# An added GpSimd drain in the tail of a 2x2 average-pooling kernel

## Chip, cores, metric

One core of a Trainium2 chip. The metric is the device time of one execution in microseconds; lower is better. All runs quoted are with a granted clock of 1.00.

## The reference

Average pooling with a 2x2 window and stride 2 on float32, 32 x 128 planes of 256 x 256, to 128 x 128 each.

```python
def setup_inputs():
    return {'x': np.random.randn(32, 128, 256, 256).astype(np.float32), 'kernel_size': 2, 'stride': 2}

def reference(x, kernel_size, stride):
    ...
            window = x[:, :, h_start:h_start + kernel_size, w_start:w_start + kernel_size].copy()
            output[:, :, i, j] = np.mean(window, axis=(2, 3))
```

1073.7 MB are read and 268.4 MB written.

## The kernel before

Each engine has its own program, tied to the others by semaphores. SyncE and ScalarE load (each the half of a tile), VectorE adds, ScalarE multiplies by 0.25, and GpSimd issues 62 stores of 4 MB each. The last 4 MB pair of tiles is stored by SyncE and the rest behind it in four smaller stores by ScalarE. The parts that matter here, with comments added:

```python
    def store(k, c):
        take(pool, scaled, 2)
        pool.dma_start(out=op[k], in_=both[c].rearrange("p t g f -> p (t g f)")).then_inc(stored[c], 16)

    def emptied_by(c, landed):
        pool.wait_ge(stored[c], landed)      # the store has landed ...
        pool.sem_inc(emptied[c])             # ... and VectorE may fill the buffer again

    with tc.tile_critical():
        # (cut: SyncE's loads, VectorE's and ScalarE's programs, the last five stores)

        store(0, 0)
        with pool.Fori(0, (pairs - 3) // 2) as i:
            for c in (1, 0):
                store(2 * i + (2 - c), c)
                emptied_by(1 - c, 16 * i + 16)
        store(pairs - 2, 1)
        for c in range(2):
            emptied_by(c, 16 * (pairs - 1) // 2)

        take(sp, tail, 16 * (len(parts) + 2))   # SyncE: all five last stores have landed
```

At the end of the critical section (line 135 in the profile) the framework makes SyncE release the other engines; each then executes a drain instruction that reports back to SyncE, and a barrier over all engines ends the program (line 290; 291 where the kernel is a line longer).

## Time and profile before

| | before |
|---|---|
| time, median of 4 runs | 3108.21 us (3107.80 to 3108.42) |
| span of the profile | 3106.8 us |
| mean DMA rate over the span | 432 GB/s |
| last landing, seen by SyncE | 3100.8 us |
| GpSimd's drain of line 135 | 3100.9 to 3106.0 us, 5127 ns |

The kernel is limited by its transfers for all but its last 6 us. In rows of a line's instructions, the columns are the line, the engine (a `q` at the end is its sequencer), the operation and how often, the durations in ns as min/median/max, and the first and last start in us. A row of the waits has the waiting engine and line, for whom, total us, times, longest us.

### The profile page before, as it was taken

To read this page: it belongs to the slowest core of one execution; us is meant where nothing else is said; L and a number is where in the kernel's file an instruction comes from. 1 tells how busy PE (TensorE), PEld (TensorE's weight loads), DVE (VectorE), ACT (ScalarE), POOL (GpSimd) and SP (SyncE) were. 2 spreads that over 40 slices of the span, in tenths; PEclk is the share of its full clock that TensorE was granted. 3 is DMA by queue.
4 is the path that set the end of the run, shared out by engine and by line. 5 is a ranking of instruction groups with operands and counts; after the bars stand their busy time and mean duration, and the time that the engine had idled before them with its cause. 6 is when DMAs were issued, how large, how long until landed. Compare 5 with 4: busy or idle time off the path is not lost. (4 is left out here: it accounts for less than half of the span.)

```text
span 3106.8 us, 2727 instructions
## 1 busy us (share of the span) xinstructions
DVE 1679.3 (54%) x260; ACT 503.1 (16%) x161; POOL 38.0 (1%) x66
## 2 busy tenths in 40 slices
DVE  5555555555555555555555555555555555555555
ACT  1111111111111111111121111211111111211111
POOL 0000000000000000000000000000000000000000
DMA  9999999999999999999999999999999999999998
GB/s 419 432 436 434 432 432 438 426 437 438 434 426 442 429 432 435 435 439 432 435 435 427 435 435 433 432 438 439 432 432 437 428 438 432 439 426 435 440 433 373
DMA packets 30449, 1342.21 MB, mean 432 GB/s; under 512 B 5232, under 2 KB 5232, under 8 KB 5488
## 3 DMA queue, kind: packets, MB, share of 16 engines
q10 hardware_dynamic: 10976, 541.07, 40.3%
q1 hardware_dynamic: 10544, 541.07, 40.2%
q0 software_dynamic: 8928, 260.05, 19.4%
q14 instruction: 1, 0.01, 0.0%
HBM read 1073.74 MB, written 268.44 MB: 432 GB/s over the span
## 5 line engine op out<-in xcount | busy, mean ns | idle before, releaser
L108 DVE TENSOR_TENSOR in_tile<-in_tile 128x8192 f32<-128x8192 f32 (+1 forms) x130 | 1112.9, 8561 | 1390.9 <-DVEq L79 1390.9
L119 ACT ACTIVATE res<-res 128x4096 f32<-128x4096 f32 x127 | 459.3, 3616 | 1975.7 <-ACTq L79 1952.0
L110 DVE TENSOR_TENSOR res<-in_tile 128x4096 f32<-128x4096 f32 x127 | 561.9, 4425 | 18.6
L119 ACT ACT_TABLE_LOAD x31 | 39.8, 1283 | 604.3 <-ACTq L79 604.3
L129 POOL DMA_DIRECT2D out_dram<-res x62 | 37.8, 610 | 2971.1 <-POOLq L79 2971.1
L119 ACT ACTIVATE in_tile<-in_tile 128x1024 f32<-128x1024 f32 (+1 forms) x3 | 4.0, 1341 | 7.3 <-ACTq L79 7.3
L110 DVE TENSOR_TENSOR in_tile<-in_tile 128x1024 f32<-128x1024 f32 (+1 forms) x3 | 4.7, 1581 | 0.4
L276 POOL MEMSET const-float32-0.0<- 128x1 f32 x1 | 0.1, 93 | 0.4 <-issue 0.4
L276 POOL MEMSET const-bfloat16-1.0<- 128x1 bf16 x1 | 0.1, 95 | 0.0
L276 POOL MEMSET const-float32-1.0<- 128x1 f32 x1 | 0.1, 93 | 0.0
L276 POOL MEMSET const-uint8-127<- 128x1 uint8 x1 | 0.1, 93 | 0.0
## 6 DMA issues: line engine op xcount, KB each, us to landing
out_dram<-res POOLq DMA_DIRECT2D x62, 4096.0 KB, 49.9
out_dram<-res SPq DMA_DIRECT2D x1, 4096.0 KB, 33.6
in_tile<-in_x_dram ACTq DMA_DIRECT2D x1, 2048.0 KB, 15.4
in_tile<-in_x_dram SPq DMA_DIRECT2D x1, 2048.0 KB, 18.1
in_tile<-in_x_dram ACTq DMA_DIRECT2D x2, 1024.0 KB, 23.1
in_tile<-in_x_dram SPq DMA_DIRECT2D x2, 1024.0 KB, 23.2
out_dram<-res ACTq DMA_DIRECT2D x1, 2048.0 KB, 16.3
in_tile<-in_x_dram ACTq DMA_DIRECT2D x127, 32.3
```

Of the source, the lines that this page charges most:

```text
L108: dve.tensor_add(out=it[:, :, 0:w], in0=it[:, :, 0:w], in1=it[:, :, w:]).then_inc(halfway)
L110: dve.tensor_add(out=dst, in0=it[:, :, 0:w:2], in1=it[:, :, 1:w:2]).then_inc(summed)
L119: act.mul(out=dst, in_=dst, mul=0.25).then_inc(sem)
L129: pool.dma_start(out=op[k], in_=both[c].rearrange("p t g f -> p (t g f)")).then_inc(stored[c], 16)
L276: nc = _bacc.Bacc("TRN2", target_bir_lowering=False, num_devices=1)
```

## The change

GpSimd knows that its last store has landed some 42 us before the others are done: in the profile before, its last wait for a store (line 133) passes at 3058.6 us, and SyncE sees the last landing at 3100.8.

```profile
L133 POOLq EVENT_SEMAPHORE  x62: 17/17/17, 111.9 to 3058.6; - x62
```

`pool.drain()` is the instruction that the framework gives GpSimd at line 135. The intent is to let GpSimd drain once in those 42 us already, and not only when SyncE releases it at the end.

```diff
         store(pairs - 2, 1)
         for c in range(2):
             emptied_by(c, 16 * (pairs - 1) // 2)
+        pool.drain()
```

## The prediction

> **What bounds the kernel now.** I read the page from its top first: busy times, the DMA row, the queues.
>
> ```profile
> span 3106.8 us, 2727 instructions
> DVE 1679.3 (54%) x260; ACT 503.1 (16%) x161; POOL 38.0 (1%) x66
> ...
> DMA  9999999999999999999999999999999999999998
> GB/s 419 432 436 434 432 432 438 426 437 438 434 426 442 429 432 435 435 439 432 435 435 427 435 435 433 432 438 439 432 432 437 428 438 432 439 426 435 440 433 373
> ...
> HBM read 1073.74 MB, written 268.44 MB: 432 GB/s over the span
> ```
>
> No engine is busy for more than 54%; the 16 DMA engines are busy in every slice and move 432 GB/s. Each byte of x is read once and each byte of the output written once, so 39 of the 40 slices are transfers. Only the last slice (373 GB/s) holds time that is not, and the change sits there. So the second reading is the end, with the chain that ended last, the waits of SyncE, and the DMA view of the last 7 us.
>
> The chain that ended last is of no help: it stops at the last ScalarE operation, 16 us before the span's end, because what follows are waits, stores and drains and not counted work. The waits of SyncE from 3050 us on carry the argument:
>
> ```profile
> SPq L79 <- SPq L79: 69.6, 3, 40.7
> SPq L135 <- POOLq L135: 4.9, 1, 4.9
> SPq L290 <- PEq L290: 0.6, 2, 0.4
> ```
>
> Each row is who waited, for whom, total, times, longest. The 40.7 us is SyncE waiting for the five last stores, up to 3100.8 us, where the output is complete. After that it waits 4.9 us for GpSimd at line 135, the end of the critical section. The instructions of that line, and of line 290, which closes the program, say what GpSimd does then (durations in ns min/median/max, then the first and last start in us):
>
> ```profile
> L135 SPq EVENT_SEMAPHORE  x3: 17/17/28, 3100.8 to 3101.1; - x3
> L135 SPq NOP  x2: 13/13/13, 0.9 to 3106.0; - x2
> L135 ACTq DRAIN  x1: 8/8/8, 3100.9 to 3100.9; - x1
> L135 POOLq DRAIN  x1: 5127/5127/5127, 3100.9 to 3100.9; - x1
> L135 DVEq DRAIN  x1: 10/10/10, 3100.9 to 3100.9; - x1
> L135 SPq DRAIN  x1: 7/7/7, 3100.9 to 3100.9; - x1
> ...
> L290 POOLq EVENT_SEMAPHORE  x4: 17/17/17, 3106.2 to 3106.7; - x4
> L290 POOLq DRAIN  x3: 34/34/77, 3106.1 to 3106.6; - x3
> L290 SPq DRAIN  x3: 7/7/7, 3106.1 to 3106.4; - x3
> ...
> L290 ACTq DRAIN  x2: 8/70/132, 3101.3 to 3106.4; - x2
> ```
>
> Four engines drain at the same moment; three need 7 to 10 ns and GpSimd 5127 ns. SyncE's NOP, which lets the program go on, starts at 3106.0 when that drain ends. So some 5 us at the end of 3108 are one GpSimd instruction in which nothing is moved: the DMA view of 3100 to 3107 us shows three packets, 0.01 MB, none on GpSimd's queue.
>
> **What the Trainium skill says.** "PSUM — Partial Sum Buffer", section "Engine vs sequencer instructions": "drain waits for the engine to go fully idle". The trace agrees in part only. GpSimd's last DMA instruction starts at 3008.9 us and takes 0.6, its last store has landed by 3058.6 us (the last wait of line 133 passes there), so by what is recorded it had been idle for 42 us when the drain began, and still it took 5.1 us. "Perfetto Trace Analysis", section "Sequencer-only Instruction (DRAIN, etc)": the reported time starts once the semaphores are satisfied. The trace agrees: the drain starts within 0.1 us of SyncE's release at 3100.8 us, and the 40 us of waiting before it are not in it; so 5127 ns is execution. "VectorE: DVE Perf Modes", section "The DRAIN you can't avoid", gives some 12 ns for a boilerplate drain on every engine: that fits 7 to 10 ns here, and not GpSimd's 34 to 5127. "DMA: Bandwidth & Descriptors", section "SWDGE vs HWDGE vs iDMA": for GpSimd's transfers software on its cores writes descriptors into rings in SBUF. No page says what a drain does with these rings. My reading, inferred, is that the first drain after transfers does overdue bookkeeping for the 62 stores of queue 0, whether or not they have landed.
>
> **The change part by part.** It removes nothing and moves nothing that exists. The built programs differ in one instruction: GpSimd has one drain more, behind its wait for the last store (line 133, at 3058.6 us) and in front of the branch out of the critical section; the drain at line 135 stays. No semaphore, transfer or tile changes, and the increment that VectorE waits for is given before the new drain.
>
> 1. The added drain. By the one measured duration it takes 5.1 us, from 3058.6 to about 3063.7 us. GpSimd has nothing to do until SyncE releases it at 3100.9 us: 42.3 us of room, 37 us of it left over. Cost on the path: 0. It could be eight times slower and stay hidden.
>
> 2. The drain at line 135. If the new one has done the bookkeeping, it costs what GpSimd's drains right after the long one cost: 34, 34 and 77 ns. It then ends at 3100.9 + 0.08, about 3101.0 us and not 3106.0.
>
> 3. What sets the end then? Not 5127 - 77 = 5050 ns saved in full, as two others come into view. SyncE's own semaphore instructions of line 135 run until 3101.1 us and its NOP follows them, so from this side the NOP moves from 3106.0 to 3101.1: 4.9 us, the wait that the row of SyncE shows. Then line 290's barrier gathers all engines. Before, the last to come was SyncE's drain, at about 3106.17 us, right after the NOP. ScalarE's first drain of line 290 starts at 3101.3 us and takes 132 ns, so it arrives at about 3101.41. It did not wait for GpSimd, so it won't be earlier. The gather is complete at 3101.4 and not at 3106.17: 4.76 us are saved. The rest of the barrier, 3106.2 to 3106.8, moves along unchanged.
>
> Sum: 3108.37 + 0 - 4.76 = 3103.61 us, 0.15% less. The span of the profile should go from 3106.8 to about 3102.0.
>
> **The rivals.** (a) The cost comes back: a drain's 5.1 us belongs to any drain of GpSimd after a long idle time, or to the one at a critical section's end, and not to unfinished bookkeeping. Then the second drain costs 5.1 us again after its 37 us of rest and the time stays 3108.4. For it: the three short drains follow the long one within 0.6 us, so none shows what a rest does. Against it: after 46 to 61 us of rest GpSimd's DMA instruction takes 608 ns, 725 at most, so waking up costs 0.1 us at best; and GpSimd's drain at the program's start, before any store, took 184 ns with four memsets around it. I give it 15%.
>
> (b) The drain waits for something outside GpSimd: for instance for all DMA engines to be quiet, or for the one packet of instruction fetch (8 KB on queue 14) that the DMA view shows between 3100 and 3107 us. If it waited for all DMA traffic, the new drain would last till about 3100.8 us, when the last store lands, and the old one would be short if nothing else remained: still near 3103.6; if 5 us must follow the last landing, nothing is gained. Against it: at 3100.9 us all transfers had landed, and the fetch is one 8 KB packet of 0.4 us that starts a microsecond into the drain. With 5%, half of it no gain.
>
> (c) The early drain disturbs what runs beside it. From 3058.6 to 3063.7 us SyncE issues the last large store and VectorE starts a tile; a drain that touches SBUF or the DMA rings could slow these. The store's issue was 0.6 us and its landing is waited for at the very end with the other stores, behind some 40 us of transfers, so even 1 us lost would be lost in full: 3104.6. I see no such sign in the trace; 10%.
>
> (d) Partly sticky: the second drain costs 1 to 2 us. Then 3104.5 to 3105.5; 5%.
>
> **Range and chances.** The middle is 3103.6. The runs of before lie within 0.37 us, and the new instruction stands behind the steady part, so I allow 1.2 us of noise downwards; upwards the range takes in (c) and (d) but not (a). So 3102.4 to 3105.8, which holds about 8 times in 10, as (a) and half of (b) take some 17%. No reading yields 2% (62 us): the whole stretch behind the last landing is 6 us. Within 2% gets 0.994, and 0.003 each side for surprises.
>
> **What would show it right or wrong.** In the profile after: a GpSimd drain on the new line, starting near 3058.6 us and near 5100 ns long (step 1); the drain of line 135 under 100 ns (step 2); SyncE's wait for GpSimd at line 135 gone or under 0.1 us, ScalarE the last at the barrier of line 290, the span near 3102.0 us (step 3). Right for the wrong reason would be a new drain that lasts until 3100 us, rival (b). Wrong it is if the drain of line 135 is still near 5 us (a), or if the last store lands later than 3100.8 us (c).

## The result, and the profile after

The changed kernel takes 3103.57 us, median of four runs (3103.24 to 3103.69), against 3108.21 us: 4.64 us less, or 0.15%. The ratio is 0.9985, with a 95% interval of 0.9968 to 1.0002. The span of the profile is 3102.0 us.

The new instruction and the lines at the end, in the profile after:

```profile
L197 POOLq DRAIN  x1: 5127/5127/5127, 3058.2 to 3058.2; - x1
```

```profile
L135 SPq NOP  x2: 13/13/13, 0.9 to 3101.1; - x2
L135 ACTq DRAIN  x1: 8/8/8, 3100.8 to 3100.8; - x1
L135 POOLq DRAIN  x1: 34/34/34, 3100.8 to 3100.8; - x1
```

```profile
L291 POOLq EVENT_SEMAPHORE  x4: 17/17/17, 3101.4 to 3101.9; - x4
L291 POOLq DRAIN  x3: 34/34/78, 3100.9 to 3101.8; - x3
L291 SPq DRAIN  x3: 7/7/7, 3101.2 to 3101.6; - x3
...
L291 ACTq DRAIN  x2: 8/70/132, 3101.3 to 3101.6; - x2
```

The reader is to see the same 5127 ns, to the nanosecond, on the new line 197 at 3058.2 us, and 34 ns in its old place. SyncE's NOP starts at 3101.1 and not at 3106.0 us. In the last fence GpSimd's semaphore instruction, which gathers the barrier, passes at 3101.4 us, when ScalarE's 132 ns drain that started at 3101.3 has ended. The waits of SyncE from 3050 us on have lost one row:

```profile
SPq L79 <- SPq L79: 69.6, 3, 40.7
SPq L291 <- PEq L291: 0.7, 2, 0.4
```

The 40.7 us for the last stores is what it was; the 4.9 us of waiting for GpSimd is gone.

### The profile page after: what moved, and what is told of

It is laid out like the page before. It is cut to its first block, busy times and chain, and to the rows that moved or that the text cites. A ratio compares the mean times of both kernels' runs of the same rounds, so it can differ in the third digit from the quotient of the medians.

```text
span 3102.0 us, 2728 instructions
## 1 busy us (share of the span) xinstructions
DVE 1679.3 (54%) x260; ACT 503.0 (16%) x161; POOL 38.0 (1%) x66
## 3 DMA queue, kind: packets, MB, share of 16 engines
q0 software_dynamic: 8928, 260.05, 19.4%
```

## Experiments

What the result alone does not tell is what those 5127 ns are: a constant, a sleep from which GpSimd wakes, code that is fetched once, or work that grows with what GpSimd has transferred. That decides when another kernel should expect them. The kernels below ran in three groups, each group on one chip beside runs of the kernel before, five rounds each: e0, e1, e3 and e4 (the kernel before 3108.31 us), e2, e5, e6 and e7 (3108.48), then e8 and e9 (3108.38).

### e0_after: the changed kernel again

> The changed kernel again, beside the kernel before on one chip, for a tighter interval. Theory (the early drain takes over the 5.1 us and hides them): 4.6 to 4.8 us less than the kernel before. If the first comparison was luck of the chip, the difference is under 2 us.

Measured: 3103.53 us (3103.45 to 3103.89) against 3108.31 us of nine runs of the kernel before: 4.78 us less, ratio 0.9984, interval 0.9970 to 0.9998. The ranges of the two kernels' runs do not overlap. The gain is real, and far below the 2% at which a kernel counts as faster here.

### e1_start: the added drain before the first store

```diff
+        pool.drain()
         store(0, 0)
```

(The drain in the tail is not there.)

> The added drain stands before GpSimd's first store, none in the tail. Theory of a debt (the cost arises from GpSimd's own transfers and the first drain behind them pays it): the added drain takes under 0.2 us, the drain of line 135 still 5.1 us, the time stays that of the kernel before (within 1 us). Rival, cold code (the first drain after the start-up pays, whatever it is for): the added drain takes about 5 us, at 1 us into the program where GpSimd has 60 us of rest, the drain of line 135 under 0.1 us, and the time falls to that of the changed kernel, 4.7 us less.

Measured: 3108.68 us (3108.48 to 3108.93), ratio 1.0001, interval 0.9987 to 1.0014. The rows of the new line and of GpSimd at line 135:

```profile
L189 POOLq DRAIN  x1: 41/41/41, 1.1 to 1.1; - x1
```

```profile
L135 POOLq DRAIN  x1: 5121/5121/5121, 3101.1 to 3101.1; - x1
```

Before any store a drain takes 41 ns, and it saves nothing later. A drain helps by where it lies, and code that is fetched by the first drain of a program is not the cost. (GpSimd's very first drain lies earlier still, at 0.4 us in every kernel here, and takes 184 ns.)

### e3_in_flight: a drain while a store is in flight

```diff
-        for c in range(2):
-            emptied_by(c, 16 * (pairs - 1) // 2)
+        emptied_by(0, 16 * (pairs - 1) // 2)
         pool.drain()
+        emptied_by(1, 16 * (pairs - 1) // 2)
```

> The tail drain stands between the waits for the last two stores: when it starts, near 3011.4 us, the last store has just been issued and 47 us of its transfer are still to come. Theory of a debt for descriptors written, which needs no landing: the drain takes 5.1 us, ends near 3016.5, the drain of line 135 takes 34 ns, the time equals that of the changed kernel within 1 us. Rival, it waits for the landing of what is in flight: the drain takes 47 to 52 us. Rival, each landing makes a debt: 5.1 us here and 5.1 us again at line 135, and the time is that of the kernel before.

Measured: 3103.51 us (3103.47 to 3103.56), ratio 0.9984; the gain is kept. The drain's row, and the one of line 135:

```profile
L196 POOLq DRAIN  x1: 52278/52278/52278, 3010.0 to 3010.0; - x1
```

```profile
L135 POOLq DRAIN  x1: 41/41/41, 3100.7 to 3100.7; - x1
```

The drain waited. By the record of landings the last store was complete at 3059.7 us, and the drain ended at 3062.3, 2.6 us behind it. So a drain of GpSimd does wait for its transfers to land. My own theory, which needed no landing, is wrong in this. Unexpected is the 2.6 us: about half of 5.1.

### e4_each_store: a drain behind each store

```diff
                 emptied_by(1 - c, 16 * i + 16)
+                pool.drain()
```

(The drain in the tail stays.)

> A drain after each wait for a store inside GpSimd's loop, and the tail drain as in the changed kernel: some 60 drains more, each with a store in flight. Theory of a fixed debt for each drain that has a transfer behind it: 60 drains of about 5.1 us, 300 us of GpSimd's time, all in its rest of some 45 us per store, and the time equals that of the changed kernel within 1 us. Rival, debt in proportion to the transfers since the last drain (5127 ns for 62 stores, 83 ns each): drains near 0.1 us. Rival, a drain disturbs the transfers or VectorE beside it, by d: 60 d more; 1 us each would be 60 us.

Measured: 3107.91 us, with a wide range, 3104.45 to 3108.99; ratio to the kernel before 0.9998, interval 0.9984 to 1.0012. The theory of a fixed debt is missed. The second expectation left out the wait for the store in flight. The third cannot be tested at this size: the 4.4 us over the changed kernel would be 0.07 us for each of 60 drains. The rows of the drain in the loop and of the one in the tail:

```profile
L194 POOLq DRAIN  x60: 45773/47447/49972, 111.6 to 2966.5; - x60
```

```profile
L198 POOLq DRAIN  x1: 132/132/132, 3062.7 to 3062.7; - x1
```

Each drain in the loop waits for the store in flight, so GpSimd can never have two stores queued. The very first one (two stores issued before it) ended 0.13 us after the second of them had landed, the rest 0.07 to 0.09 us after theirs, and none of them 5 us. A cost paid once, by the first drain behind a transfer, would have left about 2.6 us behind that first landing, as in e3, unless the wait hid it all; e8 below settles this with a second drain behind landed stores. And the tail's drain, with one landed store to answer for, took 132 ns.

This version is on average 3.6 us slower than the changed kernel in e0_after, although its last drain is short. Its trace is of its fastest run, 3104.45 us; where the others lost up to 4.5 us more isn't shown. That stays open; only the order is shown, that each store is held back until the one before has landed.

### e2_one_store_behind: one store left for the end

```diff
+        pool.drain()
         store(pairs - 2, 1)
```

(The drain in the tail is not there.)

> The added drain stands just before the last of GpSimd's stores is issued, so 61 stores lie before it and one behind it, and the drain of line 135 has that one to answer for. Theory of a fixed debt: both drains take 5.1 us, and the time is that of the kernel before within 1 us. Rival, in proportion to the number of stores: the first takes about 5.0 us, the drain of line 135 about 0.1, and the time is that of the changed kernel, 4.7 us less.

Measured: 3103.84 us (3103.66 to 3103.89), ratio 0.9985, 4.64 us less than the kernel before's 3108.48. GpSimd's drain at line 135:

```profile
L135 POOLq DRAIN  x1: 133/133/133, 3100.8 to 3100.8; - x1
```

With one store behind the last drain, the drain on the path takes 133 ns: the fixed debt is refuted, and a debt for each transfer fits. A debt that the first drain pays once would fit this run too. The added drain had a store in flight and took 49.2 us, not the 5.0 expected of it; it ended 2.55 us after that store's landing:

```profile
L194 POOLq DRAIN  x1: 49239/49239/49239, 2963.1 to 2963.1; - x1
```

### e5_late2: the tail's drain held back

The last store but one gets a semaphore of its own, `late`, and GpSimd waits for it.

```diff
+            landed = late if n == len(parts) - 2 else tail
...
+        pool.wait_ge(late, 16)
         pool.drain()
...
+        sp.wait_ge(late, 16)
-        take(sp, tail, 16 * (len(parts) + 2))
+        take(sp, tail, 16 * (len(parts) + 1))
```

> The tail drain is held back until the last store but one has landed, by the kernel before near 3098.0 us, 2.8 us before everything has landed. Theory (the drain costs only what of it reaches beyond the end of the landings): it runs from about 3098.1 to 3103.2, the drain of line 135 follows with 34 ns, the barrier at the end is complete near 3103.5 and not at 3101.4, so the time is 1.9 to 2.3 us more than the changed kernel's. Rival, the gain comes from the mere presence of the drain, not from where it lies: the same time as the changed kernel.

Measured: 3107.21 us (3107.09 to 3107.35), 3.6 us more than the changed kernel's 3103.57 and not 1.9 to 2.3. (That one ran in the first comparison; the kernel before is 0.3 us higher in this group.) The rows of the drain and of SyncE's wait:

```profile
L201 POOLq DRAIN  x1: 5127/5127/5127, 3099.4 to 3099.4; - x1
```

```profile
SPq L137 <- POOLq L137: 3.7, 1, 3.7
```

The store I waited for landed at 3099.4 us and not at 3098.0 us, so the drain began 1.4 us later than I had reckoned. With the real start the sum holds: 5.1 us from 3099.4 end at 3104.6, SyncE waits 3.7 us for it, and the span of the profile is 3105.5 us against 3102.0, 3.5 us more. What counts is the part of the drain that reaches beyond the last landing.

### e6_small and e7_one_element: one tiny transfer behind the drain

```diff
         pool.drain()
+        pool.dma_start(out=scratch[:, :], in_=xv[0:P, 0:1]).then_inc(small, 16)
+        pool.wait_ge(small, 16)
```

(Cut: the lines that make the semaphore `small` and the tile `scratch`.) The second kernel has `scratch[0:1, :]` and `xv[0:1, 0:1]` there.

> After the tail drain GpSimd issues one more transfer, 4 bytes to each of 128 partitions of a tile that nobody reads, and waits for it. Theory of a fixed debt: the drain of line 135 is back at 5.1 us, and the time is that of the kernel before within 1 us. Rival, in proportion to bytes or to the number of transfers: under 0.2 us, and the time is that of the changed kernel. Rival, cold code, paid once: 34 ns.

> As the run before, with one element of 4 bytes. Theory of a debt of fixed size per queue: 5.1 us again at line 135. Rival, in proportion to the DMA engines that moved data since the last drain (5127 ns for 16, about 320 ns each): near 0.3 us.

Measured: 3103.71 us and 3103.77 us, both with a ratio of 0.9985. GpSimd's drain of the critical section's end, with 128 elements and with one:

```profile
L139 POOLq DRAIN  x1: 133/133/133, 3100.9 to 3100.9; - x1
```

```profile
L139 POOLq DRAIN  x1: 128/128/128, 3101.3 to 3101.3; - x1
```

4 MB, 512 bytes and 4 bytes cost 133, 133 and 128 ns. The cost of one transfer barely depends on its size or on how many partitions it spans. The rival of e7, some 320 ns for each DMA engine used, falls with its 0.3 us as well.

### e8_half: one drain in the middle

```diff
-        with pool.Fori(0, (pairs - 3) // 2) as i:
-            for c in (1, 0):
-                store(2 * i + (2 - c), c)
-                emptied_by(1 - c, 16 * i + 16)
+        for i0, i1 in ((0, 15), (15, (pairs - 3) // 2)):
+            with pool.Fori(i0, i1) as i:
+                for c in (1, 0):
+                    store(2 * i + (2 - c), c)
+                    emptied_by(1 - c, 16 * i + 16)
+            if i0 == 0:
+                pool.drain()
```

(The drain in the tail is not there.)

> One drain in the middle, after 31 of GpSimd's 62 stores, none in the tail: 31 stores lie between it and the drain of line 135, which is on the path. By the runs so far a drain took 5127 ns after 62 transfers and 133 ns after one. Theory of a debt in proportion to the transfers since the last drain: (5127 - 133) / 61 = 82 ns each on 51 ns, so 31 stores make 2.59 us at line 135, and the time is 2.5 us less than that of the kernel before. Rival, a debt that is paid in full by the first drain of a program and small afterwards: 0.1 us at line 135, 4.7 us less. Rival, a size that depends on something else, such as a full ring: 5.1 us, the time of the kernel before.

Measured: 3105.79 us (3105.70 to 3106.12) against 3108.38: 2.6 us less, where 2.5 were expected; the interval of the ratio, 0.9978 to 1.0006, holds 1, but the runs of the two kernels do not overlap. GpSimd's drain and SyncE's wait for it:

```profile
L135 POOLq DRAIN  x1: 2594/2594/2594, 3100.7 to 3100.7; - x1
```

```profile
SPq L135 <- POOLq L135: 2.4, 1, 2.4
```

2594 ns were measured, 2.59 us worked out beforehand. Half the stores since the last drain, half the cost, and both rivals fall, the debt paid once too. A cost that grows with the time since the last drain would fit as well, as that is halved too; e9 decides. The drain in the middle had a store in flight and ended 1.32 us after its landing:

```profile
L196 POOLq DRAIN  x1: 51358/51358/51358, 1510.8 to 1510.8; - x1
```

### e9_twice2: twice the transfers, hardly more bytes

Against the kernel before, with no drain added:

```diff
                 store(2 * i + (2 - c), c)
+                pool.dma_start(out=scratch[0:1, :], in_=xv[0:1, 0:1]).then_inc(small, 16)
                 emptied_by(1 - c, 16 * i + 16)
+                pool.wait_ge(small, 32 * i + (16 if c else 32))
```

(Cut: the semaphore `small` and the tile `scratch`, as in e6.)

> The kernel before, no drain added, with one transfer of 4 bytes more behind each of the 60 stores in GpSimd's loop: 122 transfers in all before the drain of line 135, at 1.00 times the bytes. Theory of a debt in proportion to the number of transfers, whatever their size: 51 + 122 x 82 ns = 10.0 us at line 135, and the time is 4.9 us more than that of the kernel before, if the small transfers themselves cost nothing in the loop. Rival, in proportion to bytes or descriptors (a store has 144, the small one 17 packets at the most): 5.1 to 5.7 us, the time of the kernel before or up to 0.6 us more. Rival, a debt that stops growing at a ring's size: 5.1 us.

Measured: 3147.40 us, median of four runs (of five rounds, one gave no time), ratio 1.0121. The drain, and the packets of GpSimd's queue (number, MB, share), which were 8928 in the kernel before:

```profile
L139 POOLq DRAIN  x1: 10020/10020/10020, 3134.8 to 3134.8; - x1
```

```profile
q0 software_dynamic: 10848, 260.06, 19.2%
```

10.02 us against 10.0 expected: twice the transfers, twice the drain, though the 60 added ones move 4 bytes each. The drain does not go by packets: these grew by 22% (32 for each small transfer, and not the 17 at most of the expectation), the drain by 95%. Nor does it go by the time since the last drain, which grew by 1%. There is no upper limit up to 122 transfers. The expected time of 4.9 us more is missed, as its condition failed: the small transfers were not free. Everything had landed at 3134.8 us and not at 3100.9, so 34 us of the 39 were lost in the loop, where GpSimd now waits for each small transfer's landing, a median of 47.2 us after its issue, before it can issue the next store. Only the drain's length is read from this run.

### The law

| transfers of GpSimd since its last drain, all landed | drain, ns | run |
|---|---|---|
| 0 | 34 to 46 | after, e1, e3, e4 |
| 1 | 128 to 133 | e2, e4, e6, e7 |
| 31 | 2594 | e8 |
| 62 | 5121 to 5135 | before, after, e1, e5, e6, e7 |
| 122 | 10020 | e9 |

From the rows of 1 and 62, a drain takes 51 ns and 82 ns for each transfer: (5127 - 133) / 61 = 82. For the rows of 31 and 122 this gives 2590 and 10040 ns (2.59 and 10.0 us were put down before the runs), off by 4 and 20 ns. GpSimd's other instructions hardly count: with a semaphore wait and increment since the last drain, and no transfer, e3's drain at line 135 took 41 ns.

If a transfer is still in flight, the drain waits for it and ends some time after its landing: 1.32 us with 31 transfers since the last drain (e8's drain in the middle), 2.55 us with 61 (e2), 2.58 us with 62 (e3). That is (2.55 - 1.32) / 30 = 41 ns each, half of 82, on some 50 ns; e4's 0.13 us with two transfers and 0.07 to 0.09 with one agree. So half of the cost seems to be paid while the drain waits. What the halves are, or what the drain does for a transfer at all, no run shows.

## Why the prediction was right

- **Step 1**, the added drain costs 5.1 us and is hidden: right, 5127 ns from 3058.2 us, over at 3063.3, 37 us before SyncE's release. That nothing beside it suffers, against rival (c), holds too: the last landing was seen by SyncE at 3100.74 us, before at 3100.77, in one profile each.
- **Step 2**, the drain of line 135 falls to 34 to 77 ns: right, 34 ns. The 37 us of rest before it did not bring the cost back, so rival (a) is refuted by the changed kernel's own profile, and rival (d), a second drain of 1 to 2 us, with it.
- **Step 3**, SyncE's own instructions and then ScalarE's drain become the last, so that 4.76 us and not 5.05 are saved: right. The barrier was gathered at 3101.4 us, as forecast, and the medians differ by 4.64 us in the first comparison and 4.78 in e0_after. That the sum, 3103.61, is within 0.04 us of the measured 3103.57 is partly luck: it set out from 3108.37, the median of three runs, and the one of all four is 3108.21.
- **The reading behind the steps**, bookkeeping for each store "whether or not they have landed": half right. A cost that the first drain behind the transfers pays, with 82 ns a transfer, fits all runs; a one-time cost is excluded by e8, a constant by e2, a cost by bytes by e7 and e9, one by elapsed time or packets by e9. That it is bookkeeping, and that it has to do with the rings, stays inferred. But it does matter whether they have landed: e3's drain waited 52 us. Of rival (b), then, the part is true that a drain waits for transfers, for GpSimd's own: in e3 it ended at 3062.3 us, while the last stores of the other two queues were in flight until 3100.6. The changed kernel never met that wait, as it drains behind its wait for the last landing.

## What to carry to other kernels

If GpSimd issues many DMA transfers, expect its drain at the program's end to take 82 ns for each of them since its last drain (measured here up to 122, on one queue of one core), and all of it on the path if nothing else runs then; look in the profile for one long drain on GpSimd's sequencer behind the last landing, and for an engine that waits for it. Let GpSimd drain once more as soon as its last transfer has landed, if other engines still have more to do than that drain lasts: the instruction cost nothing here. A drain with the last transfer still in flight gained as much (e3), as GpSimd had nothing else to do. Don't drain with a transfer in flight where GpSimd has another to issue, as it blocks until the landing (46 to 50 us in e4).

## What the Trainium skill lacked or had wrong

- "DMA: Bandwidth & Descriptors", section "SWDGE vs HWDGE vs iDMA", tells how GpSimd's software writes descriptors into rings, and not that the next drain of GpSimd takes longer for each transfer behind it: 51 ns and 82 ns for each transfer since the last drain (133, 2594, 5127 and 10020 ns for 1, 31, 62 and 122), the same for 4 bytes and for 4 MB.
- "PSUM — Partial Sum Buffer", section "Engine vs sequencer instructions", says that a drain waits for the engine to go fully idle. For GpSimd that has to include the landing of its transfers (52.3 us in e3, where the instruction that issued the store took 0.6 us), and it isn't all: even 42 us after GpSimd's last landing the drain took 5127 ns.
- "VectorE: DVE Perf Modes", section "The DRAIN you can't avoid", gives about 12 ns for the boilerplate drains on all five engines, those that the runtime puts before and behind a kernel. The drains here bear lines of the kernel, so they don't refute it, but no page gives a time for them: 7 to 10 ns on SyncE, VectorE and PE, 8 ns on ScalarE but for one of 132 ns, which was the last at the closing barrier of the changed kernel, and 34 to 10020 ns on GpSimd where no transfer was in flight.
